# One unused tile of 352 bytes in SBUF ahead of X and the weight tiles

## The chip, the core and the metric

The kernel runs on one core of one Trainium2 chip. The metric is the device time of one execution in microseconds; less is better. TensorE (PE in the profile) multiplies, VectorE (DVE), ScalarE (ACT) and GpSimd (POOL) do the element-wise work, SyncE (SP) issues most transfers. SBUF is the on-chip memory from which TensorE reads both operands of a matmul; an offset below is a byte offset within each of its 128 partitions.

## The reference, cut to what matters

A decoder trunk over 256 tokens of width 2048, two layers, all in float32:

```
for i in range(2):
    hn = rms_norm(h, norm_mix_g[i])
    if i == 0: h = h + chunked_sgu_mixer(hn, a_w_in, a_g_v, a_w_s, a_b_s, a_w_out)
    else:      h = h + s5_mixer(hn, b_w_in, ..., b_w_glu)
    h = h + conv_glu_ffn(rms_norm(h, norm_ffn_g[i]), f_w_up[i], f_conv_w[i], f_conv_b[i], f_w_down[i])
return rms_norm(h, final_g)
```

Nearly all of the arithmetic is products of a 256-row activation with large weight matrices: `a_w_in` (2048x4096), `a_w_out` (2048x2048), `f_w_up` (2048x11264) and `f_w_down` (5632x2048) of two layers, `b_w_in` (2048x2048), `b_w_glu` (2048x4096).

## The kernel before, in words

Each float32 operand is cut into a high and a low part of type float32r, and each product is made of three: high by high, high by low, low by high. Activations lie in SBUF with the contracted dimension on the partitions, as 16 tiles of 128 x 512 numbers (2048 bytes a partition): the first 256 numbers are the high part of the 256 tokens, the last 256 the low part. There are two such sets. `X[0..15]` holds a normalized layer input (written by `stage_x`), `Gt[0..15]` an inner activation (written by `split_to`, and by the S5 mixer, where the list `Ys` is made of Gt tiles).

The class `Weights` streams the weights. SyncE loads tiles `w` of 1 MB (three buffers); ScalarE casts pieces of 1024 columns to `wh` (L124) and VectorE subtracts to get `wl` (L125), five buffers each.

Three forms of the product matter here. In all of them the stationary operand is loaded into TensorE by a weight load (PEld in the profile), and the moving operand streams past it.

- `group_b` (L892 to L894, tile `accb`): the stationary operand is a 128-column piece of an activation tile, the moving one 512 columns of `wh` or `wl`. L892 is high by `wh`, L893 high by `wl`, L894 low by `wh`. With X it makes the up-projections of both FFNs; with Gt it makes `a_w_out`, the down-projections and `b_w_glu`.
- `form_b` (L986 to L988): the same three products in another order of chunks. With X it makes the first half of `a_w_in` (tile `accv`), with Gt the last quarter of the last down-projection (84 matmuls).
- `form_a` (L785, L786, tile `acc`): the stationary operand is a piece of the weights, the moving one X. It makes the second half of `a_w_in` and `b_w_in`.

The names on the right of an arrow in the profile are the moving operand first, the stationary one second: `accb<-wh,Gt` streams `wh` past a piece of Gt; `acc<-X,wh` streams X past a piece of `wh`. Transposes (L820, L915) stand between the groups; in them the moving operand is the identity `ident`.

SBUF is handed out pool by pool, in the order in which tiles are first asked for. In the pool `const` come `ident`, `ones`, `cols`, `conv`, `hn`, the 16 tiles Gt, `rbc`, `rho`, `nss`, `rtok`, `tv`, `tt_`, and then the 16 tiles X, which are first asked for when the program stages them. The pool `weights` follows with three `w`, five `wh` and five `wl`, and then the pools of the single stages. The three tiles `rtok`, `tv` and `tt_` of 8 bytes take 32 each. A piece of an activation tile starts at a multiple of 512 bytes from its tile's start, and so does a piece of a weight tile, so that the offset of the tile modulo 512 is that of every operand that TensorE reads from it.

Of the kernel before, what the change touches and what calls it, by code (L numbers as in the profile page):

```python
# [9 lines left out]
F32 = mybir.dt.float32  # L10
# [7 lines left out]
P = 128  # L18
# [650 lines left out]
def tile_hybrid_trunk(  # L669
# [10 lines left out]
    const = ctx.enter_context(tc.tile_pool(name="const", bufs=1))  # L680
# [61 lines left out]
    rtok = const.tile([P, 2], F32, name="rtok")  # L742
    tv = const.tile([P, 2], F32, name="tv")
    tt_ = const.tile([P, 2], F32, name="tt_")

    scr = []
    for name, n in (
# [583 lines left out]
```

## Time and profile before

| | |
|---|---|
| median of 3 runs (lowest, highest) | 2145.45 us (2145.39, 2145.92) |
| the profiled execution | 2145.46 us, span 2143.8 us |
| PE busy | 2115.5 us, 99% of the span |
| DVE, ACT, POOL busy | 67%, 53%, 4% |
| queue of the weight transfers (q1) | 60.2% of 16 engines' span |
| mean granted TensorE clock | 0.994 |

The span runs from the first to the last instruction of the profiled execution; 1.7 us of its time lie outside it. Matmuls are pipelined, and the profile's duration of one (389 to 400 ns for 512 columns) holds a part in which the next has begun already. What a matmul costs the span is the distance from its start to the next one's start.

### The profile page before, as it was taken

To read this page: it belongs to the slowest core of one execution; us is meant where nothing else is said; L and a number is where in the kernel's file an instruction comes from. 1 tells how busy PE (TensorE), PEld (TensorE's weight loads), DVE (VectorE), ACT (ScalarE), POOL (GpSimd) and SP (SyncE) were. 2 spreads that over 40 slices of the span, in tenths; PEclk is the share of its full clock that TensorE was granted. 3 is DMA by queue.
4 is the path that set the end of the run, shared out by engine and by line. 5 is a ranking of instruction groups with operands and counts; after the bars stand their busy time and mean duration, and the time that the engine had idled before them with its cause. 6 is when DMAs were issued, how large, how long until landed. Compare 5 with 4: busy or idle time off the path is not lost.

```text
span 2143.8 us, 27328 instructions
## 1 busy us (share of the span) xinstructions
PE 2115.5 (99%) x10279; PEld 1740.3 (81%) x10279; DVE 1439.3 (67%) x2123; ACT 1134.9 (53%) x1656; POOL 90.5 (4%) x142
## 2 busy tenths in 40 slices
PE   9999999999999999999998999999999999999998
PEld 7888888888888778888887788888888888888886
DVE  5476677886896645888678766766655656546564
ACT  6544456554555534555456655555544555345553
POOL 1010000000111110000000000000000000000000
PEclk9999999999999999999999999999999999999999
DMA  8655556666777666565799986565556555555553
GB/s 277 199 180 183 188 177 199 222 218 229 215 240 232 217 207 192 189 218 198 231 254 262 271 260 196 177 207 186 176 183 198 189 186 187 181 193 181 192 177 118
DMA packets 358597, 438.59 MB, mean 205 GB/s; under 512 B 31712, under 2 KB 275520, under 8 KB 357824
## 3 DMA queue, kind: packets, MB, share of 16 engines
q1 hardware_dynamic: 349008, 407.94, 60.2%
q0 software_dynamic: 9424, 28.88, 4.6%
q8 instruction: 81, 1.33, 0.3%
q14 instruction: 52, 0.43, 0.1%
q10 hardware_dynamic: 32, 0.01, 0.0%
HBM read 414.66 MB, written 22.02 MB: 204 GB/s over the span
## 4 chain that ended last, share of the span: by engine, by line
PE 95%; DMA 3%; DVE 1%; ACT 1%; issue 0%; SPq 0%; ACTq 0%; DVEq 0%; POOLq 0%
PE accb L892 26%; PE accb L893 26%; PE accb L894 26%; PE acc L785 4%; PE acc L786 2%; PE zt L915 2%; PE accv L986 1%; PE accv L987 1%; PE accv L988 1%; DMA tab<-rd 1%; PE pt L820 1%; PE ps_x L584 1%; DMA w<-in_b_w_glu_dram 0%; DMA ud<-u 0%; ACT wh L124 0%
## 5 line engine op out<-in xcount | busy, mean ns | idle before, releaser
L125 DVE TENSOR_TENSOR wl<-w,wh 128x1024 fp32r<-128x1024 f32 (+1 forms) x721 | 879.3, 1222 | 601.9 <-ACT wh L124 597.8
L124 ACT CAST wh<-w 128x1024 fp32r<-128x1024 f32 (+1 forms) x721 | 754.4, 1050 | 769.4 <-PE accb L894 636.8
L894 PE MATMUL accb<-wh,X 128*128 128x512 f32 x1408 | 552.3, 392 | 0.0
L892 PE MATMUL accb<-wh,X 128*128 128x512 f32 x1408 | 551.7, 392 | 0.0
L893 PE MATMUL accb<-wl,X 128*128 128x512 f32 x1408 | 549.2, 390 | 0.0
L892 PE MATMUL accb<-wh,Gt 128*128 128x512 f32 x1060 | 423.2, 399 | 0.0
L894 PE MATMUL accb<-wh,Gt 128*128 128x512 f32 x1060 | 421.7, 398 | 0.0
L893 PE MATMUL accb<-wl,Gt 128*128 128x512 f32 x1060 | 421.6, 398 | 0.0
L894 PEld LDWEIGHTS accb<-wh,X 128*128 128x128 f32 x1408 | 264.3, 188 | 56.8
L893 PEld LDWEIGHTS accb<-wl,X 128*128 128x128 f32 x1408 | 264.4, 188 | 54.6
L892 PEld LDWEIGHTS accb<-wh,X 128*128 128x128 f32 x1408 | 264.4, 188 | 54.0
L894 PEld LDWEIGHTS accb<-wh,Gt 128*128 128x128 f32 x1060 | 200.3, 189 | 48.4 <-issue 0.2
L892 PEld LDWEIGHTS accb<-wh,Gt 128*128 128x128 f32 x1060 | 200.1, 189 | 48.1
L893 PEld LDWEIGHTS accb<-wl,Gt 128*128 128x128 f32 x1060 | 200.3, 189 | 47.8 <-issue 0.2
L785 PE MATMUL acc<-X,wh 128*128 128x512 f32 x512 | 185.2, 403 | 0.0
L786 PE MATMUL acc<-X,wl 128*128 128x256 f32 x512 | 145.2, 284 | 0.0
L785 PEld LDWEIGHTS acc<-X,wh 128*128 128x128 f32 x512 | 97.7, 191 | 22.0
L923 ACT ACTIVATE a<-zt,conv 128x256 f32<-128x256 f32 x176 | 94.5, 558 | 14.5 <-PE zt L915 8.2
L786 PEld LDWEIGHTS acc<-X,wl 128*128 128x128 f32 x512 | 98.3, 192 | 0.2
L942 ACT ACTIVATE z<-accb,rtok 128x512 f32<-128x512 f32 x88 | 55.8, 685 | 65.8 <-PE accb L894 65.7
L924 DVE SCALAR_TENSOR_TENSOR a<-zt,conv,a 128x255 f32<-128x255 f32 x176 | 77.6, 476 | 13.3 <-ACT a L923 13.3
L927 DVE SCALAR_TENSOR_TENSOR a<-zt,conv,a 128x254 f32<-128x254 f32 x176 | 77.1, 474 | 0.7
(299 smaller groups left out, 1407.1 us busy)
## 6 DMA issues: line engine op xcount, KB each, us to landing
w<-in_f_w_up_dram SPq DMA_DIRECT2D x352, 512.0 KB, 4.6
w<-in_f_w_down_dram SPq DMA_DIRECT2D x80, 1024.0 KB, 5.2
w<-in_b_w_glu_dram SPq DMA_DIRECT2D x64, 512.0 KB, 5.2
w<-in_a_w_in_dram SPq DMA_DIRECT2D x28, 1024.0 KB, 5.3
w<-in_a_w_out_dram SPq DMA_DIRECT2D x16, 1024.0 KB, 5.1
w<-in_b_w_in_dram SPq DMA_DIRECT2D x16, 1024.0 KB, 8.5
w<-in_f_w_down_dram SPq DMA_DIRECT2D x16, 512.0 KB, 3.7
tab<-rd SPq DMA_DIRECT2D x32, 256.0 KB, 6.9
```

The costliest lines, as they stand in the source:

```text
L124: self.nc.scalar.copy(hi[:, a:b], raw[:, o + a : o + b])
L125: self.nc.vector.tensor_tensor(lo[:, a:b], raw[:, o + a : o + b], hi[:, a:b].bitcast(F32), op=ALU.subtract)
L785: T.matmul(ps, wh, Xt[k], start=k == k_first, stop=False, skip_group_check=True)
L786: T.matmul(ps[:, NT:], wl, Xt[k][:, :NT], start=False, stop=k == ktot - 1, skip_group_check=True)
L892: T.matmul(ps[:, tt, :], xh, wh, start=k == k_first, stop=False)
L893: T.matmul(ps[:, tt, :], xh, wl, start=False, stop=False)
L894: T.matmul(ps[:, tt, :], xl, wh, start=False, stop=k == ktot - 1)
L915: T.transpose(pt[:, v * NT + tt * P : v * NT + (tt + 1) * P], z[:, tt, v * NT + q * P : v * NT + (q + 1) * P], ident,)
L923: A.activation(a[:, v], zt, AF.Identity, bias=cw[:, 3, cv : cv + 1], scale=cw[:, 2, cv : cv + 1])
L924: V.scalar_tensor_tensor(a[:, v, 1:], zt[:, : NT - 1], cw[:, 1, cv : cv + 1], a[:, v, 1:], ALU.mult, ALU.add)
L927: V.scalar_tensor_tensor(a[:, v, 2:], zt[:, : NT - 2], cw[:, 0, cv : cv + 1], a[:, v, 2:], ALU.mult, ALU.add)
L942: A.mul(z[:, tt], ps[:, tt], rtok[:, tt : tt + 1])
```

## The change

One tile that nothing reads or writes is asked for in the pool `const` behind `tt_`. It has 88 float32 numbers, 352 bytes in each partition.

```
     tv = const.tile([P, 2], F32, name="tv")
     tt_ = const.tile([P, 2], F32, name="tt_")
+    const.tile([P, 88], F32, name="pad")
```

All that lies behind it in SBUF moves up by 352 bytes: X, the weight tiles, and the tiles of the stages. What lies ahead of it stays, `ident`, `hn` and Gt among them. No instruction is added or removed, and on each of the five engines the instructions stand in the same order as before. The offsets, as the built programs have them:

| tiles | before: first tile's offset | modulo 512 | after: first tile's offset | modulo 512 |
|---|---|---|---|---|
| ident | 16512 | 128 | 16512 | 128 |
| Gt0 to Gt15 | 35648 | 320 | 35648 | 320 |
| X0 to X15 | 70112 | 480 | 70464 | 320 |
| w (3 buffers) | 102880 | 480 | 103232 | 320 |
| wh (5 buffers) | 127456 | 480 | 127808 | 320 |
| wl (5 buffers) | 147936 | 480 | 148288 | 320 |
| FFN tile z (2 buffers) | | 320, 480 | | 160, 320 |

All tiles of a set have the same offset modulo 512, since 2048, 4096 and 8192 are multiples of it.

## Rows read from the trace of the kernel before

**Rows 1.** The page: busy time of the engines, and the chain that ended last.

```profile
PE 2115.5 (99%) x10279; PEld 1740.3 (81%) x10279; DVE 1439.3 (67%) x2123; ACT 1134.9 (53%) x1656; POOL 90.5 (4%) x142
...
PE 95%; DMA 3%; DVE 1%; ACT 1%; issue 0%; SPq 0%; ACTq 0%; DVEq 0%; POOLq 0%
```

**Rows 2.** Groups by line and shape: busy us, mean ns of one, idle before.

```profile
L894 PE MATMUL accb<-wh,X 128*128 128x512 f32 x1408 | 552.3, 392 | 0.0
L892 PE MATMUL accb<-wh,X 128*128 128x512 f32 x1408 | 551.7, 392 | 0.0
L893 PE MATMUL accb<-wl,X 128*128 128x512 f32 x1408 | 549.2, 390 | 0.0
L892 PE MATMUL accb<-wh,Gt 128*128 128x512 f32 x1060 | 423.2, 399 | 0.0
L894 PE MATMUL accb<-wh,Gt 128*128 128x512 f32 x1060 | 421.7, 398 | 0.0
L893 PE MATMUL accb<-wl,Gt 128*128 128x512 f32 x1060 | 421.6, 398 | 0.0
L785 PE MATMUL acc<-X,wh 128*128 128x512 f32 x512 | 185.2, 403 | 0.0
...
L915 PE MATMUL zt<-ident,z 128*128 128x128 f32 x352 | 53.5, 272 | 0.0
L986 PE MATMUL accv<-wh,X 128*128 128x512 f32 x128 | 51.0, 398 | 0.0
...
L584 PE MATMUL ps_x<-ubd,pw 128*128 128x128 f32 x128 | 19.9, 306 | 14.1 <-DMA tab<-rd 5.6 <-DVE wl L125 2.8 <-ACT rs L621 2.8
...
L986 PE MATMUL accb<-wh,Gt 128*128 128x512 f32 x28 | 10.9, 396 | 0.0
```

**Rows 3.** PE timeline of a stretch with X, layer 0: first and last rows.

```profile
322.17 0.39 PE L893 MATMUL accb<-wl,X 128*128 128x512 f32 x1
...
343.29 0.39 PE L893 MATMUL accb<-wl,X 128*128 128x512 f32 x1
```

**Rows 4.** PE timeline of a stretch with Gt, layer 0: first and last rows.

```profile
229.79 0.40 PE L894 MATMUL accb<-wh,Gt 128*128 128x512 f32 x1
...
250.88 0.39 PE L894 MATMUL accb<-wh,Gt 128*128 128x512 f32 x1
```

**Rows 5.** PE timeline of a stretch with X, layer 1: first and last rows.

```profile
1699.02 0.40 PE L893 MATMUL accb<-wl,X 128*128 128x512 f32 x1
...
1719.88 0.39 PE L892 MATMUL accb<-wh,X 128*128 128x512 f32 x1
```

**Rows 6.** PE timeline of a stretch with Gt, layer 1: first and last rows.

```profile
1578.74 0.40 PE L894 MATMUL accb<-wh,Gt 128*128 128x512 f32 x1
...
1599.83 0.39 PE L894 MATMUL accb<-wh,Gt 128*128 128x512 f32 x1
```

**Rows 7.** Busy us (x instructions) of six 21 us windows, then clock, DMA, GB/s.

```profile
core 0: us, PE busy (x) PEld busy (x) DVE busy (x) ACT busy (x) POOL busy (x), PEclk, DMA share, GB/s
230.00:251.00 21.00, 21.00 (x91) 16.88 (x90) 15.47 (x35) 10.03 (x15) 0.00 (x0) 1.00 0.56 198
1285.00:1306.00 21.00, 21.00 (x92) 16.86 (x91) 11.81 (x11) 11.96 (x15) 0.00 (x0) 1.00 0.63 201
1579.00:1600.00 21.00, 21.00 (x91) 16.91 (x90) 10.79 (x9) 7.36 (x7) 0.00 (x0) 1.00 0.58 197
2090.00:2111.00 21.00, 21.00 (x92) 16.86 (x91) 12.20 (x14) 8.80 (x12) 0.00 (x0) 1.00 0.58 194
322.50:343.50 21.00, 21.00 (x94) 17.36 (x93) 16.66 (x38) 13.42 (x21) 0.00 (x0) 1.00 0.61 198
1699.00:1720.00 21.00, 21.00 (x94) 17.39 (x93) 13.78 (x20) 11.96 (x18) 0.00 (x0) 1.00 0.61 200
```

**Rows 8.** Groups by line: the weight cast and subtraction, and what they waited for.

```profile
L125 DVE TENSOR_TENSOR wl<-w,wh 128x1024 fp32r<-128x1024 f32 x719 | 878.0, 1224 | 595.0 <-ACT wh L124 591.0 <-DMA w<-in_b_w_in_dram 2.0 <-PE pt L820 0.3
L124 ACT CAST wh<-w 128x1024 fp32r<-128x1024 f32 x719 | 753.1, 1051 | 765.7 <-PE accb L894 636.8 <-PE acc L785 62.2 <-PE accv L988 22.8
```

More of the change, by code (lines that the diff above doesn't have):

```diff
@@ L744, in tile_hybrid_trunk @@
     tt_ = const.tile([P, 2], F32, name="tt_")
+    const.tile([P, 88], F32, name="pad")
     scr = []
```

## The prediction

> **What bounds the kernel now.** I read the page's engine line and chain first. TensorE is busy 99% of the span, and 95% of the chain that ended last is its own work [rows 1]. So time can only come out of how fast it goes from one matmul to the next, or go into that. The change moves no instruction on any engine; it moves addresses. The question is therefore whether this trace holds the same matmul at two pairs of addresses, and what each costs.
>
> It does. In `group_b` the code is the same for X and Gt: 128 columns of an activation stationary, 512 columns of `wh` or `wl` moving. The weights begin at 480 modulo 512. X begins there too, Gt at 320. The groups by line and shape give 390 to 392 ns with X and 398 to 399 with Gt, line by line [rows 2]. These durations overlap, so I went to the timeline for distances between starts, in stretches with no transposes and no idle time:
>
> - with X, layer 1: 1699.02 to 1719.88, 93 matmuls, 92 distances: 226.7 ns each [rows 5];
> - with Gt, layer 1: 1578.74 to 1599.83, 91 matmuls, 90 distances: 234.3 ns [rows 6];
> - with X, layer 0: 322.17 to 343.29, 94 matmuls, 93 distances: 227.1 ns [rows 3];
> - with Gt, layer 0: 229.79 to 250.88, 91 matmuls, 90 distances: 234.3 ns [rows 4].
>
> Could something else in the Gt stages slow TensorE? The table of windows speaks against it. It counts 91 or 92 PE instructions in 21 us in four stages that work on Gt (`a_w_out`, `b_w_glu`, the first and last thirds of the second down-projection), and 94 in two with X. In the Gt windows ScalarE is busy between 7.36 and 11.96 us and VectorE between 10.79 and 15.47; the X windows have 11.96 and 13.42, 13.78 and 16.66. The DMA share is 0.56 to 0.63 against 0.61, and the granted clock is 1.00 in all, the 2.4 GHz level [rows 7]. The X stages have as much traffic beside them or more, and are faster. The form `form_b` with Gt, other code, has 396 ns too [rows 2]. What stays constant on each side is the pair of offsets.
>
> **The change part by part.** After it X, Gt and the weights all begin at 320 modulo 512.
>
> *Matmuls on Gt.* Their stationary operand stays where it was; the moving one goes from 480 to 320, so both have the same offset, as X has before. If equal offsets are what makes 226.7, each Gt matmul falls to that distance. Their number is 3 x 1060 in `group_b` and 3 x 28 in `form_b`, 3264 [rows 2]. Of these 1440 belong to layer 0 (`a_w_out`: 4 groups x 16 chunks x 6 = 384; the down-projection: 4 x 44 x 6 = 1056), where other work lies beside them and I take the difference of layer 0, 234.3 - 227.1 = 7.2 ns: 10.4 us. The other 1824 (`b_w_glu` 768, down-projection 1056) at 234.3 - 226.7 = 7.6 ns give 13.9 us. Together 24.3 us.
>
> *What of it may not show.* Some hundred of these matmuls stand next to transposes, where the next start waits for something else, and a few dozen lie in the S5 stage, where TensorE waits for transfers (14.1 us of idle time in front of L584 [rows 2]). I take off 0.8 us. From the other side, if every matmul of `b_w_glu` gave its gain back to S5 waits, 5.8 us would go; that is my bound, and I keep it for the range.
>
> *What is late next.* Nothing, I think. At 226.7 ns one piece of 1024 weight columns lasts 12 matmuls, 2.72 us; ScalarE needs 1.05 us for it and VectorE 1.22. Most of ScalarE's wait there is for TensorE to free a buffer (636.8 us on L894), not for weights [rows 8]. The X stages already draw weights at that rate, at a DMA share of 0.61 [rows 7].
>
> *Matmuls on X.* Both operands move together from 480 to 320: 4608 in the group and vector forms, and the 1024 of `form_a`, where weights and X swap roles. Before shows no matmul with both at 320. Its nearest rows are X at 480 and 480, and Gt at 320 and 480. I take no change, since the pair stays equal. The bounds are the two rivals on X below.
>
> *Everything else behind the pad.* Transposes of `z` (352 of them) run with the identity at 128 and `z` at 320 or 480, and have one duration, 272 ns [rows 2]. They go to 160 and 320. If one in two lost or won 7.6 ns, that is 1.3 us either way. The S5, SGU and prep matmuls are few (128 of L584, say [rows 2]); by the same difference they are worth 1 us. Casts, vector work and transfers also get new addresses. They are hidden behind TensorE save for the 5% of the chain that is not PE [rows 1]; I take nothing, and a tenth of a per cent of the span, 2 us, as the bound.
>
> The sum is -24.3 + 0.8 = -23.5 us. The profiled execution took 2145.46 us, the median is 2145.45, so they may be taken as one: 2145.5 - 23.5 = 2122.0 us. By itself this case reaches from 2119 (no loss in S5, X of layer 0 at 226.7 too) to 2128 (all of `b_w_glu` hidden).
>
> **A rule against it.** The windows show the weight load of the next matmul overlapping the running one (PEld busy about 17 of 21 us beside PE at 21 [rows 7]), and Gt slower than X. The Trainium skill, "TensorE: Matmul & The Clock Gate", section "Step-by-step: what each phase is for", says that TensorE has two independent SBUF read ports, and that loading the next weights takes no read bandwidth from the running matmul. By that rule no pair of addresses could matter, and the sum would be zero: 2145.5 us. The 7.6 ns between X and Gt are not explained by it.
>
> **The rivals.**
>
> *No change.* Gt matmuls are slow because of something that comes with Gt and not with its offset: its values, or its place in SBUF, which stays. For it: X and Gt differ in more than the offset. Against it: Gt holds four different things in the four windows (gated SGU output, FFN activation, S5 output, FFN activation again) and is equally slow to a tenth of a ns where I measured. Gt stays at 234.3 and X at 226.7: 2145.5 us. The skill's rule above leads here as well.
>
> *Slower: what counts is the stationary operand's own offset, 480 good and 320 bad.* The trace of before fits this as well: stationary 480 with X, 320 with Gt, the moving one 480 in both. X then moves to the bad offset: 4608 matmuls x 7.6 ns = 35 us, and 8 more if the 1024 of `form_a` follow; Gt gains nothing. 2145.5 + 35 = 2180 us, up to 2188. Against it: 320 is a multiple of 64 and 480 only of 32, so the rounder address would be the worse one. It decides for slower as soon as X loses more than Gt gains, that is, when the distance on X grows by more than 24 / 4608 = 5 ns.
>
> *Faster still: the 480 of the weights costs something in every matmul*, with X too, because it is not a multiple of 64. At the granted 2.4 GHz, 226.7 ns are 544 cycles for 512 columns, 32 cycles or 13.3 ns more than one for each. If half of that went in all 7872 matmuls, it would be another 52 us, down to 2070. No row shows a 512-column matmul below 226.7.
>
> *Half the gain.* Gt's durations run from 392 to 400 ns in single rows, X's stand at 389 or 390. Should equal offsets at 320 only keep Gt at its better values, some 4 of 7.6 ns come back: 2133 us.
>
> **How the numbers follow.** Equal offsets in full: 0.75. Half the gain: 0.05. No change: 0.09. Slower: 0.06. Faster still: 0.05. The range 2116 to 2134 takes in the first two, 8 in 10. A measurement of this kernel can tell about 0.2% (4 us) from nothing; faster by more than that are the first, second and last cases, 0.85; within it 0.09; slower 0.06.
>
> **What would show it.** In the profile after, L892 to L894 with Gt should have means of 390 to 392 ns, and their distances 227 ns; a 21 us window should count 94 PE instructions whichever activation it works on; X rows should stand as they are; L785 and L786, L915 and L820 too; idle time in front of L584 near 14 us. It is wrong if Gt rows keep 398 ns (no change), or X rows go to 398 (slower).

## The result and the profile after

The changed kernel takes 2121.43 us (median of 4 runs, 2114.59 to 2125.28) against 2145.68 us in the same comparison; the ratio is 0.9884, 95% interval 0.9862 to 0.9906. The prediction was 2122.0 us, 2116 to 2134, and 0.85 for faster. The profiled execution of after took 2121.23 us, its span is 2119.5 us.

The pad puts one line into the file, so that L892 to L894 are now L893 to L895, L785 and L786 are L786 and L787, and L986 is L987. The page's engine line and chain, to be read beside [rows 1]:

```profile
PE 2090.7 (99%) x10279; PEld 1736.8 (82%) x10279; DVE 1439.0 (68%) x2123; ACT 1134.6 (54%) x1656; POOL 90.3 (4%) x142
...
PE 95%; DMA 3%; DVE 1%; ACT 0%; SPq 0%; issue 0%; ACTq 0%; DVEq 0%; POOLq 0%
```

TensorE's busy time fell by 24.8 us; DVE, ACT and POOL kept theirs to 0.3 us, and the number of instructions is the same on each. The groups by line and shape (busy us, mean ns of one, idle before), beside [rows 2]:

```profile
L895 PE MATMUL accb<-wh,X 128*128 128x512 f32 x1408 | 552.8, 393 | 0.0
L893 PE MATMUL accb<-wh,X 128*128 128x512 f32 x1408 | 552.1, 392 | 0.0
L894 PE MATMUL accb<-wl,X 128*128 128x512 f32 x1408 | 549.5, 390 | 0.0
L893 PE MATMUL accb<-wh,Gt 128*128 128x512 f32 x1060 | 415.8, 392 | 0.0
L895 PE MATMUL accb<-wh,Gt 128*128 128x512 f32 x1060 | 414.3, 391 | 0.0
L894 PE MATMUL accb<-wl,Gt 128*128 128x512 f32 x1060 | 414.2, 391 | 0.0
L786 PE MATMUL acc<-X,wh 128*128 128x512 f32 x512 | 184.0, 402 | 0.0
...
L916 PE MATMUL zt<-ident,z 128*128 128x128 f32 x352 | 53.5, 272 | 0.0
...
L584 PE MATMUL ps_x<-ubd,pw 128*128 128x128 f32 x128 | 20.1, 306 | 14.5 <-DMA ubd<-ud 12.9 <-DVE q L609 1.1 <-PE acc L787 0.3
...
L987 PE MATMUL accb<-wh,Gt 128*128 128x512 f32 x28 | 10.7, 389 | 0.0
```

Each Gt group lost 7.4 us and now has the duration of X; X, `form_a`, the transposes and the wait ahead of L584 stand where they stood. The timeline of PE in the second down-projection, first and last rows of a stretch with Gt, beside [rows 6]:

```profile
1559.73 0.39 PE L895 MATMUL accb<-wh,Gt 128*128 128x512 f32 x1
...
1580.81 0.39 PE L895 MATMUL accb<-wh,Gt 128*128 128x512 f32 x1
```

These are 94 matmuls and 93 distances, 226.7 ns each; before it was 234.3. And the windows of 21 us (columns as in [rows 7]; the first four in the stages on Gt, the last two on X):

```profile
230.00:251.00 21.00, 21.00 (x95) 17.36 (x94) 15.53 (x35) 9.70 (x14) 0.00 (x0) 1.00 0.55 193
1265.00:1286.00 21.00, 21.00 (x94) 17.42 (x93) 12.42 (x11) 11.94 (x17) 0.54 (x1) 1.00 0.73 233
1560.00:1581.00 21.00, 21.00 (x94) 17.42 (x93) 10.43 (x9) 8.41 (x8) 0.00 (x0) 1.00 0.64 224
2070.00:2091.00 21.00, 21.00 (x94) 17.39 (x93) 12.49 (x15) 8.89 (x13) 0.00 (x0) 1.00 0.53 176
320.00:341.00 21.00, 21.00 (x94) 17.38 (x93) 16.61 (x38) 13.55 (x22) 0.00 (x0) 1.00 0.61 199
1657.50:1678.50 21.00, 21.00 (x94) 17.34 (x93) 14.04 (x20) 11.63 (x17) 0.00 (x0) 1.00 0.59 197
```

All six now count 94 or 95 PE instructions; before, the four on Gt had 91 or 92.

Since both programs run the same matmuls in the same order, the time between two of them can be set against the time between the same two before. The Gt stages took 23.2 us less:

| stage, by matmuls | Gt matmuls | after less before, us |
|---|---|---|
| `a_w_out` | 384 | -2.7 |
| down-projection of layer 0, three parts | 1056 | -2.3, -2.3, -2.3 |
| `b_w_glu` | 768 | -1.1, -2.4, -2.3 |
| down-projection of layer 1, three parts | 1056 | -2.5, -2.9, -2.5 |
| all other stretches together | | -1.0 |

### The profile page after: what moved, and what is told of

It reads as the page before. It is cut to its first block, busy times and chain, and to the rows that moved or that the text cites. A ratio compares the mean times of both kernels' runs of the same rounds, so it can differ in the third digit from the quotient of the medians.

```text
span 2119.5 us, 27328 instructions
## 1 busy us (share of the span) xinstructions
PE 2090.7 (99%) x10279; PEld 1736.8 (82%) x10279; DVE 1439.0 (68%) x2123; ACT 1134.6 (54%) x1656; POOL 90.3 (4%) x142
## 4 chain that ended last, share of the span: by engine, by line
PE 95%; DMA 3%; DVE 1%; ACT 0%; SPq 0%; issue 0%; ACTq 0%; DVEq 0%; POOLq 0%
PE accb L893 26%; PE accb L894 26%; PE accb L895 26%; PE acc L786 4%; PE acc L787 2%; PE zt L916 2%; PE accv L987 1%; PE accv L988 1%; PE accv L989 1%; DMA w<-in_b_w_glu_dram 1%; PE pt L821 1%; DMA w<-in_b_w_in_dram 1%; DMA tab<-rd 1%; DMA ubd<-ud 0%; PE ps_x L584 0%; DMA ud<-u 0%
## 5 line engine op out<-in xcount | busy, mean ns | idle before, releaser
L895 PE MATMUL accb<-wh,X 128*128 128x512 f32 x1408 | 552.8, 393 | 0.0
L893 PE MATMUL accb<-wh,X 128*128 128x512 f32 x1408 | 552.1, 392 | 0.0
L894 PE MATMUL accb<-wl,X 128*128 128x512 f32 x1408 | 549.5, 390 | 0.0
L893 PE MATMUL accb<-wh,Gt 128*128 128x512 f32 x1060 | 415.8, 392 | 0.0
L895 PE MATMUL accb<-wh,Gt 128*128 128x512 f32 x1060 | 414.3, 391 | 0.0
L894 PE MATMUL accb<-wl,Gt 128*128 128x512 f32 x1060 | 414.2, 391 | 0.0
L895 PEld LDWEIGHTS accb<-wh,X 128*128 128x128 f32 x1408 | 264.4, 188 | 56.8
L894 PEld LDWEIGHTS accb<-wl,X 128*128 128x128 f32 x1408 | 264.6, 188 | 54.5
L893 PEld LDWEIGHTS accb<-wh,X 128*128 128x128 f32 x1408 | 264.5, 188 | 53.7
L893 PEld LDWEIGHTS accb<-wh,Gt 128*128 128x128 f32 x1060 | 199.2, 188 | 41.6
L895 PEld LDWEIGHTS accb<-wh,Gt 128*128 128x128 f32 x1060 | 199.2, 188 | 41.5 <-issue 0.2
L894 PEld LDWEIGHTS accb<-wl,Gt 128*128 128x128 f32 x1060 | 199.3, 188 | 41.1 <-issue 0.2
L786 PE MATMUL acc<-X,wh 128*128 128x512 f32 x512 | 184.0, 402 | 0.0
L787 PE MATMUL acc<-X,wl 128*128 128x256 f32 x512 | 144.8, 283 | 0.0
L786 PEld LDWEIGHTS acc<-X,wh 128*128 128x128 f32 x512 | 97.2, 190 | 21.8
L787 PEld LDWEIGHTS acc<-X,wl 128*128 128x128 f32 x512 | 97.9, 191 | 0.2
```

The lines of the kernel that those rows point to most:

```text
L786: T.matmul(ps, wh, Xt[k], start=k == k_first, stop=False, skip_group_check=True)
L787: T.matmul(ps[:, NT:], wl, Xt[k][:, :NT], start=False, stop=k == ktot - 1, skip_group_check=True)
L893: T.matmul(ps[:, tt, :], xh, wh, start=k == k_first, stop=False)
L894: T.matmul(ps[:, tt, :], xh, wl, start=False, stop=False)
L895: T.matmul(ps[:, tt, :], xl, wh, start=False, stop=k == ktot - 1)
```

## The experiments

The question left by the trace of before was which property of the offsets counts. "Difference" below is the stationary operand's offset less the moving one's. "Distance" is the mean from start to start over the matmuls of `group_b` and `form_b` that stand between two others of these forms, without the few over 260 ns: some 3155 on Gt and 4440 on X in each trace. By it before has 234.26 ns on Gt (difference -160) and 227.12 on X (0), and after 227.16 and 227.12 (both 0).

**Is 320 a good offset, or are equal ones good?** In the first run all begin at 480:

```
+    const.tile([P, 40], F32, name="padg")
     Gt = [const.tile([P, 2 * NT], F32R, name=f"Gt{k}") for k in range(KC)]
...
+    const.tile([P, 88], F32, name="pad")
```

> Gt, X and the weights all begin at 480 modulo 512 (160 unused bytes ahead of Gt, 352 behind tt_). Theory: only the difference between the two operands' offsets counts. Then Gt matmuls stand 227 ns apart as in the changed kernel, and the time is 2121 us (2115 to 2126). Rival, that 320 itself is the good offset for the stationary Gt or for the weights: Gt falls back toward 234 ns, 2140 to 2146 us.

Measured: 2122.79 us, ratio 0.9897 (0.9882 to 0.9912); distance 227.16 on Gt. Neither 320 nor 480 matters by itself. The first Gt group of this run:

```profile
L894 PE MATMUL accb<-wh,Gt 128*128 128x512 f32 x1060 | 415.4, 392 | 0.0
```

In the second only the weights move, by a tile in their own pool:

```
     wpool = ctx.enter_context(tc.tile_pool(name="weights", bufs=1))
+    wpool.tile([P, 88], F32, name="padw")
```

> X stays at 480, Gt at 320, only the weights move to 320 (the 352 unused bytes stand between X and the weights). Theory: equal offsets count, so Gt matmuls go to 227 ns (-23.5 us) and X matmuls, now 160 apart from their weights, to 234 ns (4608 x 7.3 ns = +34 us): about 2155 us, slower than both kernels. Rival, that the weights' own offset of 320 is what helped: X stays at 227 ns, about 2121 us.

Measured: 2148.05 us, ratio 1.0013 (1.0004 to 1.0023). The groups by line and shape of this run show the exchange: Gt takes X's old durations, X takes more.

```profile
L895 PE MATMUL accb<-wh,X 128*128 128x512 f32 x1408 | 562.8, 400 | 0.0
L893 PE MATMUL accb<-wh,X 128*128 128x512 f32 x1408 | 557.3, 396 | 0.0
L894 PE MATMUL accb<-wl,X 128*128 128x512 f32 x1408 | 556.5, 395 | 0.0
L893 PE MATMUL accb<-wh,Gt 128*128 128x512 f32 x1060 | 415.5, 392 | 0.0
...
L786 PE MATMUL acc<-X,wh 128*128 128x512 f32 x512 | 184.1, 401 | 0.0
```

The rival fell: X went to 233.3 ns with its own offset untouched. The size was off, 2148 and not 2155, because a difference of +160 costs 6.2 ns and not the 7.3 that the expectation put in (-160 cost 7.1); 4608 x 6.2 = 28.6 us, against 23.2 us won in the stages on Gt.

The last row limits the finding. In `form_a` the weights are the stationary operand (320 here) and X the moving one (480), so its difference in this run is -160, the one that cost Gt 7.1 ns. `form_a` did not slow down (its row after has 184.0 us and 402 ns): from one of its 512-column matmuls to the next it takes 347 ns here (a 256-column matmul lies between) and 349 to 351 in every other trace. The price by difference is therefore shown for `group_b` and `form_b` alone.

**Must the offsets agree modulo 512?** The other runs keep X and the weights together and change the size of the one pad, in bytes 96, 416, 384, 320, 480, 224, 288 and 448 in this order:

```
-    const.tile([P, 88], F32, name="pad")
+    const.tile([P, 24], F32, name="pad")
```

> X and the weights at 64 modulo 512, Gt at 320: the difference of Gt to its weights is 256. X keeps equal offsets, 227 ns. If the offsets must agree modulo 512, Gt stands near 234 ns and the time near 2145 us. If modulo 256, 128 or 64 is enough, Gt stands at 227 ns and the time is near 2121 us.

> X and the weights at 384 modulo 512, Gt at 320: a difference of 64. If the offsets must agree modulo 512, 256 or 128, Gt stands near 234 ns and the time near 2145 us. If modulo 64 is enough (the 160 of the kernel before is 32 modulo 64), Gt stands at 227 ns, near 2121 us.

Measured: 256 apart costs nothing (227.17 ns; 2120.75 us, ratio 0.9887, 0.9872 to 0.9902), so agreement modulo 512 is more than is needed. -64 costs little (228.99 ns; 2124.61 us, 0.9904, 0.9889 to 0.9919). That left two theories, multiples of 64 or closeness, for four more:

> X and the weights at 352, Gt at 320: stationary less moving is -32. Theory A: a difference that is a multiple of 64 is cheap (0 and 256 gave 227.2 ns, -64 gave 229.0), an odd multiple of 32 is dear (-160 gave 234.3, 160 on X 233.3): Gt near 234 ns, about 2145 us. Theory B: the price grows with the size of the difference modulo 256: Gt near 228 ns, about 2124 us.

> X and the weights at 288, Gt at 320: stationary less moving is +32. Theory A (odd multiples of 32 are dear): Gt near 233 to 234 ns, 2141 to 2145 us. Theory B (the price grows with the size of the difference): near 228 ns, about 2124 us.

> X and the weights at 448, Gt at 320: stationary less moving is -128. Theory A (multiples of 64 are cheap): Gt at 227 to 229 ns, 2121 to 2126 us. Theory B (the price grows with the size of the difference modulo 256, and 128 is the largest): Gt at 232 ns or more, 2138 us or more.

> X and the weights at 192, Gt at 320: stationary less moving is +128, the same as -128 if only the difference modulo 256 counts. Then its Gt distance is that of the run with -128 to a few tenths of a ns. Theory A: 227 to 229 ns, 2121 to 2126 us. Theory B: 232 ns or more, 2138 us or more.

Both fell. 32 apart, on either side, costs nearly as much as 160 (233.29 and 233.27 ns), so closeness does not help; 128 apart, a multiple of 64, costs 232.47 on either side. That the two with 128 agree to a hundredth of a ns is what a period of 256 asks for. Two more runs tried sign and period:

> X and the weights at 256, Gt at 320: stationary less moving is +64. If the distance depends on the size of the difference and not on its sign (as 32 and 128 did), Gt stands at 229.0 ns as with -64, about 2125 us. If the sign matters, another value between 227 and 235 ns.

> X and the weights at 416, Gt at 320: stationary less moving is -96, which is 160 modulo 256. If only the difference modulo 256 counts, Gt stands at 233.3 ns, as X did when its difference was 160, and not at the 234.3 of -160: 2140 to 2143 us. If the full period is 512, the value is free; 230 ns or less would show it.

The period held: -96 has 233.34 ns, as +160 had on X (233.33), and not the 234.26 of -160. The sign matters: +64 has 233.34, -64 had 228.99. The timeline of the run with +64, Gt in the second down-projection, first and last of 91 matmuls:

```profile
1559.77 0.39 PE L894 MATMUL accb<-wl,Gt 128*128 128x512 f32 x1
...
1580.77 0.39 PE L894 MATMUL accb<-wl,Gt 128*128 128x512 f32 x1
```

That is 90 distances, 233.3 ns. Tiles are placed at multiples of 32 bytes, so a difference of 16 needs Gt cut from one tile, 16 bytes behind its start:

```
-    Gt = [const.tile([P, 2 * NT], F32R, name=f"Gt{k}") for k in range(KC)]
+    Gts = const.tile([P, KC * 2 * NT + 4], F32R, name="Gts")
+    Gt = [Gts[:, 512 * k + 4 : 512 * k + 516] for k in range(KC)]
...
-    const.tile([P, 88], F32, name="pad")
+    const.tile([P, 80], F32, name="pad")
```

> As the changed kernel, but the 16 tiles Gt are cut from one tile 16 bytes behind its start, so that Gt begins at 336 and X and the weights at 320: a difference of +16. If any difference but a multiple of 256 costs, Gt stands at 230 ns or more and the time is 2130 us or more. If 16 is too little to matter, 227.2 ns and 2121 us.

Measured: 231.36 ns, but this mean hides two levels. The timelines of two stretches of this run, in `b_w_glu` and in the second down-projection, first and last rows:

```profile
1274.83 0.39 PE L895 MATMUL accb<-wl,Gts 128*128 128x512 f32 x1
...
1295.91 0.39 PE L895 MATMUL accb<-wl,Gts 128*128 128x512 f32 x1
```

```profile
1559.73 0.40 PE L896 MATMUL accb<-wh,Gts 128*128 128x512 f32 x1
...
1580.97 0.40 PE L894 MATMUL accb<-wh,Gts 128*128 128x512 f32 x1
```

The first has 93 distances of 226.7 ns, as at equal offsets, the second 91 of 233.4, as with 32. Over the whole run the Gt matmuls stand at one or the other for stretches of dozens to hundreds, about three in ten at the lower. So 16 bytes cost nothing in some stretches and as much as 32 in others; what decides between them stays open. All values of the Gt distance (X stays at 227.1 to 227.2 in each of these runs):

| difference | distance, ns | median, us | ratio to before, 95% interval |
|---|---|---|---|
| 0 (after) | 227.16 | 2121.43 | 0.9884 (0.9862, 0.9906) |
| 256 | 227.17 | 2120.75 | 0.9887 (0.9872, 0.9902) |
| -64 | 228.99 | 2124.61 | 0.9904 (0.9889, 0.9919) |
| 16 | 231.36 (mean of two levels) | 2133.56 | 0.9949 (0.9926, 0.9971) |
| 128 | 232.47 | 2138.60 | 0.9976 (0.9965, 0.9987) |
| -128 | 232.47 | 2138.18 | 0.9966 (0.9952, 0.9979) |
| 32 | 233.27 | 2140.76 | 0.9986 (0.9972, 1.0000) |
| -32 | 233.29 | 2137.44 | 0.9969 (0.9957, 0.9980) |
| 64 | 233.34 | 2130.43 | 0.9930 (0.9907, 0.9952) |
| -96 | 233.34 | 2135.92 | 0.9971 (0.9948, 0.9994) |
| -160 (before) | 234.26 | | 1 |

**A row that doesn't fit, and a faster kernel.** With +64 Gt wins only 0.9 ns, 3264 x 0.9 = 3 us, yet the time fell by 13. The same matmuls set against each other put nearly all of it into the S5 stage: from the matmul that starts at 1056 us in the trace of before to the one at 1211 us, before took 155.0 us, this run 140.1. After took 152.9, and the others 147.6 to 152.6. In that run X, the weights and the S5 tiles `ubd`, `u`, `pw`, `tab`, `qw` and `yt` begin at multiples of 256 bytes. The idle time in front of L584 there:

```profile
L584 PE MATMUL ps_x<-ubd,pw 128*128 128x128 f32 x128 | 18.5, 290 | 4.6 <-DMA ubd<-ud 3.8 <-issue 0.7
```

The table of transfers of before (KB each, median us to landing), and of that run:

```profile
w<-in_f_w_up_dram SPq DMA_DIRECT2D x352, 512.0 KB, 4.6
...
w<-in_b_w_in_dram SPq DMA_DIRECT2D x16, 1024.0 KB, 8.5
...
tab<-rd SPq DMA_DIRECT2D x32, 256.0 KB, 6.9
```

```profile
w<-in_f_w_up_dram SPq DMA_DIRECT2D x352, 512.0 KB, 4.3
...
w<-in_b_w_in_dram SPq DMA_DIRECT2D x16, 1024.0 KB, 6.8
...
tab<-rd SPq DMA_DIRECT2D x32, 256.0 KB, 5.8
```

They land sooner. The clock has a part in it too. The windows from the one matmul to the other (columns as in [rows 7]), of before, of the run with +64 and of the last run below, and one more of before:

```profile
1056.09:1211.06 154.97, 140.82 (x960) 120.39 (x959) 124.28 (x172) 91.78 (x135) 9.64 (x18) 0.94 1.02 262
1055.71:1195.79 140.08, 134.88 (x960) 115.57 (x959) 122.65 (x170) 89.86 (x132) 9.61 (x18) 0.99 0.98 285
1047.60:1189.03 141.43, 133.53 (x960) 114.32 (x959) 123.07 (x170) 89.90 (x132) 9.60 (x18) 1.00 0.99 284
1128.00:1131.40 3.40, 3.12 (x12) 2.96 (x13) 3.22 (x5) 1.73 (x4) 0.00 (x0) 0.50 0.93 247
```

In before the granted clock fell four times to 0.50, the 1.2 GHz level, for 17.0 us in all, each time during or just behind a wait of 1.9 to 3.7 us in front of L584 (a fifth wait, of 2.5 us, had no fall behind it). With +64 it fell once, for 3.4 us, and in the last run not at all. An estimate of the 15 us that the run with +64 saved there: 9.5 us are waits in front of L584 (14.1 less 4.6), and the rest is work done at the higher clock, which at half speed for 13.6 us more could cost up to 6.8.

The last run joins both: multiples of 256 for the transfers, and a difference of 256 for the matmuls.

```
+    const.tile([P, 48], F32, name="padg")
     Gt = [const.tile([P, 2 * NT], F32R, name=f"Gt{k}") for k in range(KC)]
...
+    const.tile([P, 24], F32, name="pad")
```

> Gt begins at 0 modulo 512 (192 unused bytes ahead of it), X, the weights and the S5 tiles at 256, where the run with the difference +64 had them. Theory: two effects that add. Gt's difference to its weights is 256, so Gt matmuls stand 227.2 ns apart; and the S5 stage, which took 15 us less than before in the run with +64 while Gt gained only 3 us there, is shorter because the transfers write to offsets that are multiples of 256. Then 2130 less 20 (3264 x 6.2 ns), about 2110 us (2105 to 2114), and the w transfers of f_w_up land in 4.3 us. Rival: that run's S5 stage was short by the run-to-run spread alone; then about 2121 us, as the changed kernel. The Trainium skill, DMA: Bandwidth & Descriptors, section How a descriptor splits into AXI transactions, says that a descriptor that does not start at a multiple of 256 bytes costs an extra piece, which would favour the first.

Measured: 2108.10 us (2107.68 to 2110.65, 5 runs), ratio 0.9832 (0.9819 to 0.9846), faster than both kernels. The distance on Gt is 227.11 ns, the S5 stretch takes 141.4 us. Its transfers, and L584:

```profile
w<-in_f_w_up_dram SPq DMA_DIRECT2D x352, 512.0 KB, 4.3
...
w<-in_b_w_in_dram SPq DMA_DIRECT2D x16, 1024.0 KB, 7.1
...
tab<-rd SPq DMA_DIRECT2D x32, 256.0 KB, 6.1
```

```profile
L584 PE MATMUL ps_x<-ubd,pw 128*128 128x128 f32 x128 | 17.6, 280 | 6.6 <-DMA ubd<-ud 3.9 <-DMA tab<-rd 1.7 <-DVE q L609 0.9
```

The Trainium skill, "DMA: Bandwidth & Descriptors", section "How a descriptor splits into AXI transactions", says that the first transaction of a descriptor that does not start at a multiple of 256 bytes starts at the boundary below, and that the bytes before the start are fetched and not used. The traces agree in direction (4.3 us to landing in the two where w begins at such a multiple, 4.5 or 4.6 in the twelve where it does not), but the page speaks of what is fetched, and here only the addresses written to moved; that this is the cause is not shown. Which of the tiles has to be aligned for it, the weights or those of S5, I did not separate.

## Why the prediction was right, point by point

*What bounds the kernel.* Right: 24.8 us less of PE busy time became 24.3 us less of span.

*Gt at the distance of X.* Right in mechanism and nearly in size. The step gave 24.3 us; the stages on Gt took 23.2 us less. Of these some 1.4 are not the offsets': around 1200 us, eight Gt matmuls stand up to 427 ns apart in before, at the clock of 0.50, and 224 to 298 in after. That leaves near 22 us. That the pair counts and neither operand alone is shown by the run with all at 480 and the one that moved the weights alone. One reading put beside it carries nothing as it was read: `form_b` has 396 to 397 ns with Gt, but also 394 to 398 with X at equal offsets [rows 2]. Its distances do carry: 234.3 ns with Gt and 227.4 with X.

*The split by layers.* Wrong reason, small effect. I put 227.1 against 226.7 ns on X down to other work in layer 0. In after the X stretch at 1657.19 of layer 1, with the same work beside it, shows 227.1 ns:

```profile
1657.19 0.39 PE L894 MATMUL accb<-wl,X 128*128 128x512 f32 x1
...
1677.86 0.39 PE L895 MATMUL accb<-wh,X 128*128 128x512 f32 x1
```

(92 matmuls, 91 distances.) So these 0.4 ns are not the price of other work; what sets them stays open. Term by term, layer 0 gave 9.7 us where 10.4 was reckoned, the rest 13.6 where it was 13.9, or about 12.2 without the part of the clock.

*What may not show.* I took off 0.8 us; 1.1 was missing, or some 2.5 without the part of the clock. So the median's lying 0.6 us from the forecast is luck in part: the Gt stages gave a little less than reckoned, other stretches gave 1.0 us that was not reckoned, and the four runs of after span 10.7 us.

*X, transposes, other matmuls.* Right at nothing: X has 227.12 ns before and after, L916 272 ns, and all other stretches together moved by 1.0 us.

*Transfers.* I allowed 2 us for new addresses of hidden work. For this pad that holds: 152.9 us in the S5 stretch against 155.0; of these 2 us at most 0.5 are the offsets of its 67 Gt matmuls (67 x 7.1 ns), and some 1.4 are the clock named above. As a bound it was too small: other addresses shorten the stretch by 14 us. It is also where the runs of one kernel may differ; the wait ahead of L584 was for `tab` in before and for `ubd` in after, while the idle time there, 14.1 and 14.5 us, is nearly the same. What spreads the runs of after is not separated.

*The rivals.* No change: refuted, Gt's values stayed and its distance fell. Slower, by the stationary's own offset: refuted, X at 320 keeps 227.12 ns. Faster still, by a multiple of 64: refuted, X stands at 227.1 with offsets of 256, 320 and 480 alike. Half the gain at equal offsets: did not occur.

The same matmul takes 227.2 or 234.3 ns a start by the offsets of its operands. The rule of the Trainium skill, "TensorE: Matmul & The Clock Gate", section "Step-by-step: what each phase is for", on two independent read ports does not cover that. That the load of the next stationary operand is the partner is argued from its overlap with the running matmul and not shown; next and running stationary have one offset in these stages. Why `form_a` pays nothing stays open too.

## What to carry to other kernels

Where TensorE is busy all the time, compare the distance between starts of equal matmuls on different tiles; a difference of 3% with the same code is a reason to print the tiles' SBUF offsets. In products of the form of `group_b`, let stationary and moving tiles of float32r agree modulo 256 bytes, and try tiles that transfers write to at multiples of 256: unused tiles of 192 and 96 bytes gave 1.7% here. Before trusting a total, set the same instructions of two traces against each other by stage, since one pad acts on more than one thing.

## What the runs showed that I had not expected

The price is not monotone: 32 bytes of difference cost 6.1 ns a matmul, -64 only 1.8, 128 cost 5.3, 256 nothing; 16 bytes cost nothing or about 6.6, by stretch. And +64 and -64 differ (6.2 against 1.8 ns), while +32 and -32 do not; +128 and -128, which are one difference modulo 256, agree. `form_a` shows no price at -160.

Waits in the S5 stage can cost more than their own time: the granted clock fell during or behind them, for 17.0 us in before, 3.4 with +64 and not once in the fastest kernel.
